# Two model blocks on one core: GpSimd arithmetic out of the first mixer, decay rows read back from DRAM, output transposed inside the last product

## The chip, the core and the metric

The kernel runs on one core of a Trainium2 chip. The core has five instruction streams: TensorE (PE, matrix products; its weight loads are shown apart as PEld), VectorE (DVE), ScalarE (ACT), GpSimd (POOL), and SyncE (SP), which here only issues transfers from device memory (DRAM) through 16 DMA engines. Operands lie in on-chip memory (SBUF) with 128 partitions; PE writes to a second memory, PSUM, which is made of banks. Each stream runs in order and waits for the others through semaphores. The metric is device time in microseconds (us), the median of several runs.

## The reference

256 tokens of width 1024 pass through two models in a row; all weights are float32.

```python
# first model, one layer
h = rmsnorm(x) * (1 + scale_m) + shift_m            # six vectors from c_act @ w_ada + b_ada
x = x + gate_m * hybrid_mixer(h)                    # retention + two gated recurrences, then w_out
x = x + gate_f * hierarchical_moe(rmsnorm(x)...)    # 32 experts, two chosen per token
x = rmsnorm(x)
# second model: layer 0 (state space mixer + dilated attention, then a gated feed-forward),
# layer 1 (conformer convolution, then a gated feed-forward); six vectors per layer as above
a_cs = cumsum(dt * A)                               # per head, inside chunks of 128 tokens
decay = exp(where(causal, a_cs[l] - a_cs[s], -inf))
y = (C B^T * decay) @ (x * dt) + (carried state)    # 32 heads, 2 chunks
return rms_norm(x, final_norm_g)
```

## The kernel before

All activations lie with the features on the partitions and the 256 tokens along the free axis. Weights stream in as 1 MB tiles (`rawa`, five buffers, loaded by SP in a fixed order); each 128x1024 piece is split by ACT (`whi`, line 211) and DVE (`wlo`, line 212) into a rounded part and a remainder, and each product takes three PE instructions per 128x128 block (lines 653 to 655 in `dense_B`, 727 to 729 in `dense_A`). Order is written out by hand: generators in a list `pipes` are advanced by one step ("tick") at fixed places of a dense product, twice in each 128-column tile of `z`, so the side work of the mixers is interleaved with the products' instructions. There is no scheduler behind it: an instruction that waits holds up all behind it on its engine.

**The first mixer** runs from about 40 to 264 us: products `fg`, `gq`, `vt`, `rqk`, `gate`, with the recurrences (`recur`), `retention` and `rotate` as side work. `recur` computes exponentials into a tile `X` (ACT) and multiplies seven levels of it by `gq` (DVE, line 976) and by `gk` (POOL, line 977); then 32x32 products on PE, whose results DVE masks (lines 1007 to 1011) and ACT copies (lines 1016 to 1018). `rotate` multiplies by sine (DVE, 902) and by cosine (POOL, 903) and adds the two (DVE, 904). Between the tiles the six modulation vectors are computed. For one third of the first model's (set (0, 2)) this is done in `ada_pooled`: POOL multiplies a 1 MB tile by the vector and adds it up in four instructions (lines 491 to 495), then two small PE products (line 503) sum over the partitions. All other sets go through `ada`: four PE products of 128x512 per tile (line 524).

**The experts** follow: their weights go to nine buffers `rawb`, which lie where the first mixer's tiles lay, so their loads can't start before the mixer has ended, and to the five `rawa` buffers.

**The state space mixer** of the second model is side work of the product `z` (16 tiles, n = 0 to 15, about 640 to 742 us): `ssd(j)` handles two heads. For each pair POOL spreads the log decays over a matrix (`Lm`, line 1720), PE forms the running sums with a triangular constant (line 1740; the second chunk's alone, line 1728), ACT takes exponentials (`M`, `e`, lines 1742 and 1744), DVE multiplies with the group's C B^T (`cbm`, line 1745), and PE forms the output (1751) and what the first chunk hands on (1753), from a third copy `xe` (POOL, 1734). DVE then combines (1754 to 1757), multiplies by the gate (`yz`, 1760), and splits the result with ACT (1768, 1769); POOL adds up squares (1762, 1764).

**The end**: after the last product `dn1`, mean square, reciprocal root (`rsqrt`, lines 606 to 611, on DVE), the root spread along the free axis by PE (`along`, 617), eight multiplications (2137), sixteen PE transposes (2143), four copies (2145, 2147) and two DMAs to the output.

Of the kernel before, what the change touches and what calls it, by code (L numbers as in the profile page):

```python
# [269 lines left out]
def _trace(ctx, tc, A, out, dbg, stop):  # L270
# [63 lines left out]
    more = spread([(0, 1, i) for i in range(8)] + [k for i in range(8) for k in ((0, 2, i), (1, 0, i))])  # L334
# [152 lines left out]
    def ada_pooled(l, b, q):  # L487

        raw = ws.get(("ada", l, b, q))
        col = 0 if l == 0 else 8  # L490
# [3 lines left out]
        t = const.tile([128, T], FT, name="sq", tag="sq", bufs=2)  # L494
        G.tensor_tensor(t, raw[:, 0], raw[:, 1], op=OP.add)
        ws.free(("ada", l, b, q))
        bias = vcol["b_ada"] if l == 0 else vcol["ada_b_2"][:, 48 * l - 48:48 * l]
        n = b * 16 + 2 * q

        def end():  # L500
            ps = mis()
            for j in range(2):
                P.matmul(ps[:, j:j + 1], t[:, j * 128:(j + 1) * 128], ones_1, start=True, stop=True)
            V.tensor_tensor(mods[l][:, n:n + 2], ps[:, 0:2], bias[:, n:n + 2], op=OP.add)
        later(9 if l else 8, end)
# [452 lines left out]
    def recur(u, heads, voff0, ot0, i):  # L958
# [13 lines left out]
        for li, m in enumerate(LEVELS):  # L972
# [4 lines left out]
            G.tensor_tensor(xv[:, :, :, 0, :], xv[:, :, :, 0, :], kv[:, :, :, 0, :], op=OP.mult)  # L977
# [548 lines left out]
    def ffn(l, mod, gain, sq, fill):  # L1526
        with ExitStack() as lx:
# [34 lines left out]
        return sq  # L1562

    with ExitStack() as l2:
# [151 lines left out]
        def ssd(j):  # L1716

            g, yj = j // 4, y[j // 4][:, j % 4]
            Lm = wk.tile([128, 2, 2, 128], FT, name="Lm", tag="Lm", bufs=2)
            G.tensor_tensor(Lm, SLb[:, None, None].to_broadcast([128, 2, 2, 128]),  # L1720
                            dA[:, :, 2 * j:2 * j + 2][:, :, :, None].to_broadcast([128, 2, 2, 128]), op=OP.mult)
            yield True
            yield True
# [441 lines left out]
```

## Time and profile before

| | us |
|---|---|
| median of 3 runs | 1557.94 |
| lowest, highest | 1554.55, 1560.27 |
| profiled execution | 1556.02 |
| its span, first to last instruction | 1554.2 |
| PE busy in it | 1380.5 (89%) |
| DVE busy | 898.1 (58%) |
| ACT busy | 633.0 (41%) |
| POOL busy | 359.2 (23%) |

The span is what the trace covers; 1.8 us lie around it. Busy times of different engines overlap. PE is the engine with the least slack, but its share is a mean over stages with different limits: in the experts' stage it waits for weights, in the feed-forward products it never stops.

### The profile page before, as it was taken

Reading aid. Unit: us, or ns where it says so; the run is one execution under the profiler, and the core shown is the slowest. Engines: PE = TensorE matmul, PEld = TensorE weight load, DVE = VectorE, ACT = ScalarE, POOL = GpSimd, SP = SyncE. Lnnn points to the kernel's source line nnn. Section 1 sums busy time; section 2 is a strip of 40 time slices with the busy share of each in tenths; the row PEclk is TensorE's granted clock in tenths of the full one; section 3 lists DMA queues with packets and bytes.
Section 4 is the critical chain, followed back from the end, with each engine's and each line's share of the span. In section 5 each row is a group of like instructions: output and inputs, shape, how many; then the busy total and the mean of one; then the engine's idle time right before and its main releaser. Section 6 shows DMA issues by size and latency. Waiting matters only on the chain.

```text
span 1554.2 us, 29404 instructions
## 1 busy us (share of the span) xinstructions
PE 1380.5 (89%) x12145; PEld 1184.7 (76%) x12145; DVE 898.1 (58%) x1683; ACT 633.0 (41%) x1117; POOL 359.2 (23%) x402
## 2 busy tenths in 40 slices
PE   3978699796687689999998899999999998999997
PEld 1757578763343389888997786899998887899997
DVE  3676666631112287877664566665555787765544
ACT  2633223320101257544443454454443766554432
POOL 3163642100000011154256203900000574000000
PEclk9998789896978889999999899999999999999998
DMA  8883456979999985655799976776557564877540
GB/s 309 295 284 125 154 163 217 361 293 418 374 417 419 359 140 152 209 180 170 178 179 168 234 200 204 208 207 178 174 182 217 177 190 136 244 193 188 176 150 28
DMA packets 283613, 344.00 MB, mean 221 GB/s; under 512 B 18249, under 2 KB 258368, under 8 KB 265552
## 3 DMA queue, kind: packets, MB, share of 16 engines
q1 hardware_dynamic: 272016, 335.33, 67.9%
q0 software_dynamic: 10848, 5.33, 3.5%
q8 instruction: 97, 1.59, 0.4%
q10 hardware_dynamic: 608, 1.39, 0.2%
q14 instruction: 44, 0.36, 0.1%
HBM read 340.63 MB, written 1.10 MB: 220 GB/s over the span
## 4 chain that ended last, share of the span: by engine, by line
PE 51%; DMA 9%; DVE 7%; ACT 3%; POOL 2%; issue 2%; POOLq 0%; SPq 0%; DVEq 0%; ACTq 0%
PE acc L653 14%; PE acc L654 14%; PE acc L655 14%; DMA rawa<-in_hy_w_in_dram 3%; DMA rawb<-in_expert_w_up_dram 3%; DVE wlo L212 2%; PE adaps L524 2%; POOL c L2029 1%; PE acc L1407 1%; DMA rawb<-in_expert_w_gate_dram 1%; PE mis L1740 1%; DMA rawa<-in_expert_w_up_dram 1%; DMA rawa<-in_expert_w_gate_dram 1%; ACT whi L211 1%; DVE q L1695 1%
## 5 line engine op out<-in xcount | busy, mean ns | idle before, releaser
L212 DVE TENSOR_TENSOR wlo<-rawa,whi 128x1024 fp32r<-128x1024 f32 (+1 forms) x303 | 378.2, 1252 | 252.2 <-ACT whi L211 251.4
L653 PE MATMUL acc<-hhi,whi 128*128 128x256 f32 (+2 forms) x1728 | 513.7, 297 | 9.4 <-ACT hhi L643 5.4
L654 PE MATMUL acc<-hlo,whi 128*128 128x256 f32 (+2 forms) x1728 | 500.0, 289 | 1.6 <-DVE hlo L649 1.2
L655 PE MATMUL acc<-hhi,wlo 128*128 128x256 f32 (+2 forms) x1728 | 498.1, 288 | 0.1
L653 PEld LDWEIGHTS acc<-hhi,whi 128*128 128x128 f32 (+2 forms) x1728 | 338.6, 196 | 45.1 <-issue 24.0
L211 ACT ACTIVATE whi<-rawa 128x1024 fp32r<-128x1024 f32 (+1 forms) x304 | 313.5, 1035 | 145.1 <-PE acc L654 105.2
L654 PEld LDWEIGHTS acc<-hlo,whi 128*128 128x128 f32 (+2 forms) x1728 | 338.9, 196 | 5.0 <-DVE hlo L649 4.2
L655 PEld LDWEIGHTS acc<-hhi,wlo 128*128 128x128 f32 (+2 forms) x1728 | 339.3, 196 | 0.5 <-DVE wlo L212 0.3
L653 PE MATMUL acc<-ghi,whi 128*128 128x256 f32 x352 | 99.6, 283 | 0.0
L654 PE MATMUL acc<-glo,whi 128*128 128x256 f32 x352 | 99.6, 283 | 0.0
L655 PE MATMUL acc<-ghi,wlo 128*128 128x256 f32 x352 | 99.6, 283 | 0.0
L1407 PE MATMUL acc<-rawb,X 128*32 128x256 f32 x576 | 63.9, 459 | 18.7 <-DMA rawb<-in_expert_w_gate_dram 10.9
L524 PE MATMUL adaps<-rawa,cs 128*32 128x512 f32 (+1 forms) x576 | 69.9, 587 | 6.0 <-DMA rawa<-in_w_ada_dram 6.0
L1979 POOL TENSOR_SCALAR dg<-cst,pcols 128x128 f32<-128x128 f32 x75 | 53.1, 726 | 84.1 <-PE acc L655 84.1
L1415 DVE TENSOR_TENSOR sq<-sq,acc 128x256 f32<-128x256 f32 x8 | 3.4, 421 | 117.0 <-PE acc L1407 117.0
L653 PEld LDWEIGHTS acc<-ghi,whi 128*128 128x128 f32 x352 | 67.6, 192 | 0.0
L654 PEld LDWEIGHTS acc<-glo,whi 128*128 128x128 f32 x352 | 67.6, 192 | 0.0
L655 PEld LDWEIGHTS acc<-ghi,wlo 128*128 128x128 f32 x352 | 67.6, 192 | 0.0
L1407 PE MATMUL acc<-rawa,X 128*32 128x256 f32 x320 | 45.4, 514 | 20.5 <-DMA rawa<-in_expert_w_up_dram 9.9
L1407 PEld LDWEIGHTS acc<-rawb,X 128*32 128x32 f32 x576 | 28.3, 131 | 43.3 <-DMA rawb<-in_expert_w_gate_dram 16.0
L1471 POOL TENSOR_TENSOR X<-X 128x256 f32<-128x256 f32 x5 | 3.9, 782 | 235.9 <-ACT X L1468 235.6
L1793 POOL DMA_DIRECT2D bt<-rbd x64 | 50.8, 806 | 31.7 <-DMA bt<-rbd 30.2
(598 smaller groups left out, 2415.0 us busy)
## 6 DMA issues: line engine op xcount, KB each, us to landing
rawa<-in_ada_w_dram SPq DMA_DIRECT2D x48, 1024.0 KB, 5.1
rawa<-in_w_ada_dram SPq DMA_DIRECT2D x24, 1024.0 KB, 8.2
rawa<-in_ffn_w_gate_dram SPq DMA_DIRECT2D x44, 512.0 KB, 4.0
rawa<-in_ffn_w_up_dram SPq DMA_DIRECT2D x44, 512.0 KB, 5.3
rawa<-in_hy_w_in_dram SPq DMA_DIRECT2D x20, 1024.0 KB, 7.4
rawa<-in_hy_w_in_dram SPq DMA_DIRECT2D x40, 512.0 KB, 7.5
rawb<-in_expert_w_gate_dram SPq DMA_DIRECT2D x18, 1024.0 KB, 19.9
rawb<-in_expert_w_up_dram SPq DMA_DIRECT2D x18, 1024.0 KB, 16.2
```

The source lines that it names most:

```text
L211: self.nc.scalar.activation(hv, src, AF.Copy)
L212: (engine or self.nc.vector).tensor_tensor(lv, src, hv.bitcast(FT), op=OP.subtract)
L524: P.matmul(ps[32 * g:32 * g + 32, :], cs[:, col + k:col + k + 1].to_broadcast([128, 32]), raw[:, k, g * w:(g + 1) * w], start=(q + k == 0) ...
L653: P.matmul(ps, wh, xh, start=start, stop=False)
L654: P.matmul(ps, wh, xl, start=False, stop=False)
L655: P.matmul(ps, wl, xh, start=False, stop=stop)
L1407: P.matmul(ps[32 * i:32 * i + 32, :256], X[:, kt, o:o + 32], half(raws[i], kt // 4)[:, kt % 4 * 256:kt % 4 * 256 + 256], start=(kt == 0), ...
L1695: V.scalar_tensor_tensor(a_[:, s_:], ps[:, :T - s_], cw[:, i:i + 1], a_[:, s_:], op0=OP.mult, op1=OP.add)
L1740: P.matmul(sg_[:, o:o + 128], Lm[:, c, a], Ub, start=True, stop=True)
L1793: nc.gpsimd.dma_start(bt[:, a, o + 64 * g:o + 64 * g + 64], bass.AP(tensor=rbd.tensor, offset=base + 511 + 127 * g, ap=[[0, 2], [1, 64], [ ...
L1979: G.tensor_scalar(diag[n][:, i], ident, tap(i, n), None, op0=OP.mult)
L2029: G.tensor_tensor(c2, c2, pr_, op=OP.add)
```

## The change

Three stages are rewritten. In the first mixer, set (0, 2) of the modulation goes through `ada` like the others, the `gk` multiplication moves from POOL to DVE, and `rotate` multiplies by cosine on DVE. In `ssd` the running sums of all heads are computed once in `softplus`, written to DRAM (`cumd`), and read back two heads at a time as rows repeated over the 128 partitions (`load_rows`, a POOL-issued DMA of 256 KB, two pairs ahead); decays come from them by an added bias, a maximum and an exponential. `Lm`, `xe`, the products 1728, 1740 and 1753 and the combination 1754 and 1757 are gone; two extra exponentials, two maxima on ACT, two on DVE, a 128x256 product on DVE and two on PE come in. At the end the gain is multiplied and the tile transposed inside `dn1`, tile by tile, and the root is applied as a per-token scale in the copies out of PSUM.

```diff
-    POOLED = {(0, 2)}
-    more = spread([(0, 1, i) for i in range(8)] + [k for i in range(8) for k in ((0, 2, i), (1, 0, i))])
+    more = spread([(l, b, i) for l, b in ((0, 1), (0, 2), (1, 0)) for i in range(8)])
-    def ada_pooled(l, b, q):
-        raw = ws.get(("ada", l, b, q))
...
-        G.tensor_tensor(raw, raw, cs[:, col:col + 8, None].to_broadcast([128, 8, 256]), op=OP.mult)
-        G.tensor_tensor(raw[:, 0:4], raw[:, 0:4], raw[:, 4:8], op=OP.add)
-        G.tensor_tensor(raw[:, 0:2], raw[:, 0:2], raw[:, 2:4], op=OP.add)
...
-        G.tensor_tensor(t, raw[:, 0], raw[:, 1], op=OP.add)
...
         P.matmul(p2[:, :T], cc("pm"), q, start=True, stop=True)
-        t1 = tmp("t1")
-        V.tensor_tensor(t1, p2[:, :T], sinT, op=OP.mult)
-        G.tensor_tensor(q, q, cosT, op=OP.mult)
-        V.tensor_tensor(rqk[:, n], t1, q, op=OP.add)
+        V.tensor_tensor(p2[:, :T], p2[:, :T], sinT, op=OP.mult)
+        V.tensor_tensor(rqk[:, n], rqk[:, n], p2[:, :T], op=OP.add)
...
         S.activation(q, ps[:, :T], AF.Copy)
+        V.tensor_tensor(rqk[:, n], ps[:, :T], cosT, op=OP.mult)
...
-            G.tensor_tensor(xv[:, :, :, 0, :], xv[:, :, :, 0, :], kv[:, :, :, 0, :], op=OP.mult)
+            V.tensor_tensor(xv[:, :, :, 0, :], xv[:, :, :, 0, :], kv[:, :, :, 0, :], op=OP.mult)
...
+            for c in range(2):
+                P.matmul(ps[:, 32 + 32 * c:64 + 32 * c], Ub, dA[:, c], start=True, stop=True)
+                P.matmul(ps[:32, 128 + 128 * c:256 + 128 * c], dA[:, c], Ub, start=True, stop=True)
+            V.tensor_copy(cum, ps[:, :96].rearrange("p (c h) -> p c h", c=3))
...
+            S.activation(pdt, ps[:32, 128:384], AF.Copy, scale=-1.0)
+            nc.gpsimd.dma_start(cumd, pdt)
+            rows.extend(load_rows(j) for j in range(2))
...
+        def load_rows(j):
+            tag, bufs = (("M", MB), ("Lm", 2))[j % 3 // 2]
+            R = wk.tile([128, 2, 2, 128], FT, name="R", tag=tag, bufs=bufs)
+            nc.gpsimd.dma_start(R.rearrange("p a c t -> p (a c t)"), bass.AP(
+                tensor=cumd.tensor, offset=cumd.offset + 2 * j * T, ap=[[0, 128], [1, 2 * T]]))
+            return R
...
-            Lm = wk.tile([128, 2, 2, 128], FT, name="Lm", tag="Lm", bufs=2)
-            G.tensor_tensor(Lm, SLb[:, None, None].to_broadcast([128, 2, 2, 128]),
...
-            yield True
+            M = rows.popleft()
+            if j < 14:
+                rows.append(load_rows(j + 2))
+            M01 = wk.tile([128, 2, 128], FT, name="M01", tag="M01", bufs=2)
+            for a in range(2):
+                h = 2 * j + a
+                S.activation(M01[:, a], M[:, a, 1], AF.Exp, bias=cum[:, 0, h:h + 1], scale=-1.0)
+                for c in range(2):
+                    if a:
+                        S.activation(M[:, a, c], M[:, a, c], AF.Relu, bias=cum[:, 1 + c, h:h + 1])
+                    else:
+                        V.tensor_scalar(M[:, a, c], M[:, a, c], cum[:, 1 + c, h:h + 1], 0.0, op0=OP.add, op1=OP.max)
+            yield True
+            S.activation(M, M, AF.Exp, scale=-1.0)
             yield True
...
-            for a in range(2):
-                P.matmul(pe[64 * a:64 * a + 64, 256:384], dA[:, 1, 2 * j + a:2 * j + a + 1].to_broadcast([128, 64]), Ub,
-                         start=True, stop=True)
...
-                    P.matmul(sg_[:, o:o + 128], Lm[:, c, a], Ub, start=True, stop=True)
...
-            S.activation(M, sg_.rearrange("p (c a t) -> p c a t", c=2, a=2), AF.Exp)
...
-            S.activation(e1, pe[:, 256:384], AF.Exp)
-            V.tensor_tensor(M, M, cbm[:, g, 0::2][:, :, None].to_broadcast([128, 2, 2, 128]), op=OP.mult)
+            V.tensor_tensor(M, M, cbm[:, g, 0::2][:, None].to_broadcast([128, 2, 2, 128]), op=OP.mult)
+            V.tensor_tensor(M01, M01, cbm[:, g, 1][:, None].to_broadcast([128, 2, 128]), op=OP.mult)
...
-            P.matmul(py[:, 256:384], xe, cbm[:, g, 1], start=True, stop=True)
-            V.tensor_tensor(e1, e1, py[:, 256:384], op=OP.mult)
+            for a in range(2):
+                P.matmul(py[64 * a:64 * a + 64, 128:256], xd[:, 0, 64 * a:64 * a + 64], M01[:, a], start=False,
+                         stop=True)
...
-            V.tensor_tensor(yt[:, 128:], yt[:, 128:], e1, op=OP.add)
...
+            turned_ = [mis() for _ in range(4)] if fin is not None else []
...
+                if fin is not None:
+                    xg = wk.tile([128, T], FT, name="xg", tag="t0", bufs=2)
+                    V.tensor_scalar(xg, xT[:, n], fin[:, n:n + 1], None, op0=OP.mult)
+                    later(2, lambda: turn_out(n, xg))
...
-        rst = rstd_of(sq)
-        for k in range(8):
-            V.scalar_tensor_tensor(xT[:, k], xT[:, k], vcol["final_norm_g_2"][:, k:k + 1], rst, op0=OP.mult, op1=OP.mult)
+        ps = acc()
+        sq.mean(ps)
+        r = rsqrt(ps[:, 0:2])
...
+            S.activation(ot[:, :512], turned_[2 * c], AF.Copy, scale=r[:, c:c + 1])
+            V.tensor_scalar(ot[:, 512:], turned_[2 * c + 1], r[:, c:c + 1], None, op0=OP.mult)
+            (nc.scalar if c else nc.sync).dma_start(out[0, c * 128:(c + 1) * 128, :], ot)
```

How this moves instructions is seen best on the two engines that PE waits for. On DVE in the first mixer, where `X` of the second recurrence is multiplied, seven rows stood between `X<-X,gq` and the masking of the 32x32 products:

```order
L971 TENSOR_TENSOR X<-X,gq 128x128
L976 TENSOR_TENSOR X<-X,gq 128x2x64
L976 TENSOR_TENSOR X<-X,gq 128x2x2x32
L976 TENSOR_TENSOR X<-X,gq 128x2x4x16
L976 TENSOR_TENSOR X<-X,gq 128x2x8x8
L976 TENSOR_TENSOR X<-X,gq 128x2x16x4
L976 TENSOR_TENSOR X<-X,gq 128x2x32x2
L976 TENSOR_TENSOR X<-X,gq 128x2x64
L1007 TENSOR_TENSOR dt__1003<-mis,l1c 128x384
```

With the change the same stretch of DVE holds both multiplications (its last rows; line numbers are those of the changed file, where 976 is 949 and 1007 is 980):

```order
L949 TENSOR_TENSOR X<-X,gq 128x2x8x8
L950 TENSOR_TENSOR X<-X,gk 128x2x8x8
L949 TENSOR_TENSOR X<-X,gq 128x2x16x4
L950 TENSOR_TENSOR X<-X,gk 128x2x16x4
L949 TENSOR_TENSOR X<-X,gq 128x2x32x2
L950 TENSOR_TENSOR X<-X,gk 128x2x32x2
L949 TENSOR_TENSOR X<-X,gq 128x2x64
L950 TENSOR_TENSOR X<-X,gk 128x2x64
L980 TENSOR_TENSOR dt__1002<-mis,l1c 128x384
```

So fourteen DVE instructions stand ahead of the masking in place of seven. On ACT in `z`, one step before (from the split of a pair's result, `yh`, to the next weight piece, `whi`; `t` is the tile's own evacuation):

```order
L1768 ACTIVATE yh_7725<-yz,pcols 128x256
L1773 ACTIVATE t_9143<-acc 128x256
L1742 ACTIVATE M<-mis 128x512
L1744 ACTIVATE e_9173<-mis 128x128
L211 ACTIVATE whi_9191<-rawa 128x1024
```

and with the change:

```order
L1768 ACTIVATE yh_7689<-yz,pcols 128x256
L1736 ACTIVATE R<-R 128x512
L1773 ACTIVATE t_8962<-acc 128x256
L1729 ACTIVATE M_8984<-R,cum 128x128 x2
L1732 ACTIVATE R<-R,cum 128x128 x2
L211 ACTIVATE whi_9004<-rawa 128x1024
```

The large exponential now stands ahead of the tile's evacuation instead of behind it, and the two small ones and the maxima, which read the rows from DRAM, stand ahead of the weight split.

## Rows read from the trace of the kernel before

**Rows 1.** windows: stretch, length, busy PE PEld DVE ACT POOL, PEclk, DMA share, GB/s

```profile
100.00:200.00 100.00, 71.40 (x1171) 57.79 (x1161) 67.88 (x85) 26.43 (x71) 52.19 (x37) 0.80 0.46 145
200.00:264.00 64.00, 59.93 (x635) 48.49 (x634) 48.09 (x81) 18.12 (x41) 28.33 (x16) 0.89 0.58 188
264.00:530.00 266.00, 197.63 (x1835) 123.72 (x1835) 73.37 (x193) 38.09 (x67) 5.64 (x7) 0.83 0.94 382
640.00:740.00 100.00, 100.00 (x848) 82.03 (x848) 76.24 (x143) 44.20 (x86) 46.25 (x60) 1.00 0.56 180
```

**Rows 2.** longest waits of PE from 40 to 240 us: total, times, longest

```profile
PE acc L727 <- ACT vtok L929: 13.1, 1, 13.1
PE mis L1072 <- DVE rqk L904: 9.7, 1, 9.7
...
PE mis L944 <- DVE mt L1074: 2.4, 1, 2.4
```

**Rows 3.** timeline of DVE, 100 to 125 us: start, duration, instruction

```profile
101.60 3.69 DVE L970 TENSOR_TENSOR X<-X,gk 128x128 f32<-128x128 f32 x1
...
105.41 8.68 DVE L976 TENSOR_TENSOR X<-X,gq 128x128 f32<-128x128 f32 x7
```

**Rows 4.** timeline of POOL in the same stretch

```profile
100.56 4.58 POOL L491 TENSOR_TENSOR rawa<-rawa,cs 128x2048 f32<-128x2048 f32 x1
```

**Rows 5.** line 976 alone: durations in ns, least/median/most

```profile
L976 DVE TENSOR_TENSOR X<-X,gq x28: 278/570/3687, 91.9 to 189.1; 128x128 f32<-128x128 f32 x28
```

**Rows 6.** line 904 alone, likewise

```profile
L904 DVE TENSOR_TENSOR rqk<-t,rq x6: 425/654/3809, 85.0 to 213.7; 128x256 f32<-128x256 f32 x6
```

**Rows 7.** timeline of DVE, 180 to 230 us

```profile
183.11 8.46 DVE L976 TENSOR_TENSOR X<-X,gq 128x128 f32<-128x128 f32 x7
...
224.88 2.45 DVE L607 TENSOR_SCALAR nw<-nw 128x12 int32<-128x12 int32 x1
```

**Rows 8.** timeline of SyncE's DMA queue, 262 to 268 us

```profile
263.76 3.98 SPq L183 DMA_DIRECT2D rawb<-in_expert_w_gate_dram  x4
```

**Rows 9.** timeline of PE in `z`, 679 to 692 us

```profile
679.30 1.06 PE L524 MATMUL adaps<-rawa,cs 128*32 128x512 f32 x8
...
683.35 0.66 PE L1751 MATMUL mis<-M,xd 128*64 128x128 f32 x8
683.94 0.49 PE L1753 MATMUL mis<-cbm,xe 128*128 128x128 f32 x2
684.26 0.38 PE L1726 MATMUL mis<-cst,y 128*128 128x128 f32 x2
684.57 0.44 PE L1728 MATMUL mis<-cst,dA 128*64 128x128 f32 x4
...
685.86 0.36 PE L653 MATMUL acc<-hhi,whi 128*128 128x256 f32 x1
...
691.58 1.06 PE L524 MATMUL adaps<-rawa,cs 128*32 128x512 f32 x8
```

**Rows 10.** timeline of all engines at the end of the program

```profile
1542.41 0.16 DVE L611 SCALAR_TENSOR_TENSOR nw<-nw 128x2 f32<-128x2 f32 x1
...
1549.44 0.69 DVE L2145 COPY ot<-mis 128x512 f32<-128x512 f32 x1 [1.01 <-PE mis L2143]
```

**Rows 11.** groups of instructions by line: busy us in all, mean ns of one

```profile
L503 PE MATMUL mis<-epsc,sq 128*128 128x1 f32 x32 | 4.7, 252 | 0.0
```

**Rows 12.** timeline of DVE in `z`

```profile
677.73 0.48 DVE L1769 SCALAR_TENSOR_TENSOR ylo<-yz,pcols,yh 128x256 fp32r<-128x256 f32 x1 [0.58 <-ACT yh L1768]
...
678.47 0.28 DVE L1754 TENSOR_TENSOR e<-e,mis 128x128 f32<-128x128 f32 x1
```

**Rows 13.** line 1745 alone, least/median/most ns

```profile
L1745 DVE TENSOR_TENSOR M<-M,cbm x16: 691/798/1068, 644.1 to 735.9; 128x512 f32<-128x512 f32 x16
```

**Rows 14.** timeline of ACT in `z`

```profile
679.40 0.60 ACT L1742 ACTIVATE M<-mis 128x512 f32<-128x512 f32 x1 [1.44 <-PE mis L1740]
```

**Rows 15.** line 1789, attention bias loads issued by POOL

```profile
DMA to landing us min/median/max: 5.8/10.3/12.9
```

More of the change, by code (lines that the diff above doesn't have):

```diff
@@ L309, in plan_ada @@
         w, c = ada_w[l], b * 2048
-        if (l, b) in POOLED:
-            src, shape = w[:, c + kt * 256:c + kt * 256 + 256].rearrange("(k p) n -> p k n", p=128), (8, 256)
-        elif (l, b) in HALVED:
+        if (l, b) in HALVED:
             h, q = divmod(kt, 4)
@@ L485, in _trace @@
     ada_ps = {}
-    def ada_pooled(l, b, q):
-        raw = ws.get(("ada", l, b, q))
-        col = 0 if l == 0 else 8
-        G.tensor_tensor(raw, raw, cs[:, col:col + 8, None].to_broadcast([128, 8, 256]), op=OP.mult)
-        G.tensor_tensor(raw[:, 0:4], raw[:, 0:4], raw[:, 4:8], op=OP.add)
-        G.tensor_tensor(raw[:, 0:2], raw[:, 0:2], raw[:, 2:4], op=OP.add)
-        t = const.tile([128, T], FT, name="sq", tag="sq", bufs=2)
-        G.tensor_tensor(t, raw[:, 0], raw[:, 1], op=OP.add)
[L496 to L505, printed above, removed]
     def ada(l, b, kt):
-        if (l, b) in POOLED:
-            ada_pooled(l, b, kt)
-            return
         h = 2 if (l, b) in HALVED else 1
@@ L533, in ada_ends @@
     def ada_ends(l, b, kt):
-        return (l, b) not in POOLED and kt % (4 if (l, b) in HALVED else 8) == (3 if (l, b) in HALVED else 7)
+        return kt % (4 if (l, b) in HALVED else 8) == (3 if (l, b) in HALVED else 7)
     def ada_end(l, n, w, sb):
@@ L1524, in _trace, with ffn @@
     hl1.close()
-    def ffn(l, mod, gain, sq, fill):
+    def ffn(l, mod, gain, sq, fill, fin=None):
         with ExitStack() as lx:
@@ L1645, in softplus @@
             P.matmul(ps[:, :32], cc("SLk"), dA[:, 0], start=True, stop=True)
-            S.activation(dec, ps[:, :32], AF.Exp)
-        dec = wk.tile([128, 32], FT, name="dec")
+            for c in range(2):
+                P.matmul(ps[:, 32 + 32 * c:64 + 32 * c], Ub, dA[:, c], start=True, stop=True)
+                P.matmul(ps[:32, 128 + 128 * c:256 + 128 * c], dA[:, c], Ub, start=True, stop=True)
+            V.tensor_copy(cum, ps[:, :96].rearrange("p (c h) -> p c h", c=3))
+            pdt = wk.tile([32, T], FT, name="pdt", tag="t1", bufs=2)
+            S.activation(pdt, ps[:32, 128:384], AF.Copy, scale=-1.0)
+            nc.gpsimd.dma_start(cumd, pdt)
+            rows.extend(load_rows(j) for j in range(2))
+        cum = wk.tile([128, 3, 32], FT, name="cum")
+        cumd = dr.tile([32, T], FT, name="cumd")
+        rows, MB = deque(), 4
+        def load_rows(j):
[4 more added lines that the diff above has]
+            return R
         y = [wk.tile([128, 4, T], FT, name="y", tag="y4", bufs=5) for _ in range(4)]
@@ L1718, in ssd @@
             g, yj = j // 4, y[j // 4][:, j % 4]
-            Lm = wk.tile([128, 2, 2, 128], FT, name="Lm", tag="Lm", bufs=2)
-            G.tensor_tensor(Lm, SLb[:, None, None].to_broadcast([128, 2, 2, 128]),
-                            dA[:, :, 2 * j:2 * j + 2][:, :, :, None].to_broadcast([128, 2, 2, 128]), op=OP.mult)
+            M = rows.popleft()
[5 more added lines that the diff above has]
+                S.activation(M01[:, a], M[:, a, 1], AF.Exp, bias=cum[:, 0, h:h + 1], scale=-1.0)
+                for c in range(2):
+                    if a:
+                        S.activation(M[:, a, c], M[:, a, c], AF.Relu, bias=cum[:, 1 + c, h:h + 1])
+                    else:
+                        V.tensor_scalar(M[:, a, c], M[:, a, c], cum[:, 1 + c, h:h + 1], 0.0, op0=OP.add, op1=OP.max)
             yield True
+            S.activation(M, M, AF.Exp, scale=-1.0)
             yield True
@@ L1821, in scores @@
                 for a, ps in enumerate(pss):
-                    s = wk.tile([128, 384], FT, name="s", tag="M", bufs=4)
+                    s = wk.tile([128, 384], FT, name="s", tag="M", bufs=MB)
                     st = wk.tile([128, 4], FT, name="st", tag="st", bufs=4)
```

31 lines of the change are left out of this document (8 added, 23 removed).

## The prediction

> **What bounds the kernel now.** I first cut the program into its stages with the view of stretches, because the shares of the whole hide different limits. Between 100 and 200 us, in the first mixer, PE is busy 71.4 of 100 us at a mean granted clock of 0.80, the DMA engines 46%; from 200 to 264 us PE is busy 59.9 of 64 at 0.89; DVE and POOL are both half busy or more [rows 1]. So neither PE nor the transfers set this stage: 28.6 + 4.1 = 32.7 us are idle, and 71.4 x 0.20 + 59.9 x 0.11 = 20.9 us of PE's busy time are lost to the clock. The view of waits says to whom: 13.1 us in one wait for the evacuation of `vtok` by ACT, 9.7 us for `rqk` of DVE, 2.4 us for `mt` of DVE [rows 2].
>
> I followed the first of these back on the timelines. ACT stood behind copies that need DVE's masking, and DVE spent 101.60 to 114.09 us on lines 970 to 976: 3.69 us in one instruction, 8.68 us in seven [rows 3], while POOL worked on a modulation tile [rows 4]. These are not slow instructions in themselves: line 976 takes 0.278 us at best and 3.687 at worst on the same shape [rows 5], line 904 from 0.425 to 3.809 [rows 6]. The long ones lie where POOL runs a long one. The same is seen ahead of the second wait, 8.46 us for seven, and in a tiny 128x12 instruction of `rsqrt` that takes 2.45 [rows 7]. The Trainium skill (SBUF — State Buffer, "SBUF: two separate sides") says that DVE and GpSimd share one pair of ports and that whoever starts holds it for the whole instruction when the DVE instruction reads two SBUF operands. The trace agrees: 3.69 us of DVE beside 4.58 us of POOL.
>
> Whether a shorter mixer shortens the program is read from what follows. The experts' loads are issued from 263.76 us on, when the mixer's memory falls free [rows 8], and from there to 530 us the DMA engines are busy 94% [rows 1]. That stage is bound by transfers whose start hangs on the mixer's end, so it should move as a block.
>
> In `z` (640 to 740 us) PE is busy without a gap at full clock [rows 1]; two steps, with one modulation tile, take 691.58 - 679.30 = 12.28 us, a step 6.14 [rows 9]. At the end, 1542.57 us (last instruction of `rsqrt`) to 1550.13 (last copy) is a chain with nothing beside it [rows 10].
>
> **The change, part by part.** *First mixer.* POOL's long instructions leave. DVE's `X` block becomes fourteen multiplications at most 0.278 each, 3.9 us, with the two before them some 4.5 in all. At the first wait that replaces 12.5 us: 8.0 saved of 13.1. At the second, 8.46 becomes 3.9 (4.6 saved), and line 904, at worst 3.81, becomes 0.43 (3.4): 8.0 of 9.7. At the third `rsqrt` gets its 2.3 back. The gain is 18.3 us of idle time. The clock fell around these waits; if the loss goes in the proportion of the idle time, 18.3/32.7 of 20.9 is 11.7 us; I take that, with nothing and all of 20.9 as ends. Against it: eight modulation tiles go to PE at 1.06 us each [rows 9], 8.5 us, while line 503 with 4.7 us leaves [rows 11]: 3.8 us more. The third instruction of `rotate` on DVE (0.43 six times) lies on an engine that is then far from full, and costs nothing unless DVE is again late at `rqk`. Sum 18.3 + 11.7 - 3.8 = 26.2 us. Bounds: 14.5 with no clock given back, about 40 where nearly every wait goes.
>
> *State space stage.* On PE a step loses line 1753 (684.26 - 683.94 = 0.32 us) and lines 1728 and 1740 (685.86 - 684.57 = 1.29), and gains two products like the four of line 1751 (0.59 / 2 = 0.30) [rows 9]: 1.31 us less, 4.83 a step, 21.0 us in sixteen. But then DVE is next. It is busy 76.2 us in 100 [rows 1], 4.68 a step. Lines 1754 and 1757 leave (0.28 each), the two maxima on 128 columns cost at most the same; the 128x256 product costs 0.42, as line 904 at its best [rows 6]; without POOL's `Lm` the product with `cbm` comes nearer its best, 0.69 for 0.80 [rows 13]. That is 4.99, and 0.58 us are DVE's wait for ACT between `yz` and `ylo` [rows 12], which stays: 5.57 a step. DVE can end the stage about one step behind PE (5 us, 0.3 a tile) and make it up under the next product, where it only splits weights. So 5.27, and 16 x 0.87 = 13.9 us saved. The upper bound is PE's 21. The lower bound is nothing: the large exponential (0.60 on ACT [rows 14]) now stands between `yh` and the tile's evacuation, and if all of it is added to DVE's loop the step is 6.17.
>
> The rows come by POOL-issued DMA, an operation the stage did not have. They are asked for two steps ahead, some 10.5 us. The nearest row is the bias loads of 129 KB, which land after 5.8 to 12.9 us, median 10.3, under a much fuller DMA [rows 15]; in `z` the engines are 56% busy [rows 1], so I take the lower end for 256 KB in long pieces, 6 us, and no wait. By the formula of the Trainium skill (DMA: Bandwidth & Descriptors, "Anatomy of one DMA — SWDGE (gpsimd) path") it would be an estimated 2.6 us; its 2.3 us for the bias loads is far under what the trace shows, so the rows decide. Either leaves this sum as it is. What is queued behind a late row on ACT is the weight split, and PE waits for that.
>
> *End.* From the root to the last copy there remain two copies on each of ACT and DVE, 2 x 0.69 = 1.4 us in place of 7.56 [rows 10]: 6.1 saved. But the transposes enter a product in which PE has no gap: a pair costs 0.31 (684.57 - 684.26 [rows 9]), six pairs 1.9; the last two pairs and the multiplication by the gain come before the mean, about 1.0. Net 3.2 us; bounds 2 and 6.
>
> **Sum.** 26.2 + 13.9 + 3.2 = 43.3 us from the profiled execution's 1556.0 gives 1512.7. The median of the runs shown is 1.9 above that execution; I add half of it and forecast 1514.
>
> **The rivals.**
> - *The first mixer finds its next wait, or the clock is not given back.* In favour: the chains ACT-DVE-PE there are long, and a copy that waits holds up the evacuations behind it. Against: three waits hold 25 us of the 33. The mixer gives 14.5: 1525.
> - *DVE and ACT set the step in `z`*, as in the lower bound above. For: the order of ACT; against: the maxima and splits may hide in the slack. `z` gives 0 to 5: 1523 to 1528. With the first rival together, about 1537.
> - *The mixer's gain is lost before the experts.* If the expert loads did not start sooner, the time would be 1540. Against it stands that their start is a release of memory [rows 8].
> - *More than I count:* nearly all idle time and clock of the first mixer come back and `z` runs at PE's 4.83: about 1490.
> - *The other side: rows that land late.* With a landing time of L the step can't be under L / 2. At 12.9 us it is 6.45, `z` loses 5 us and the time is about 1532. It is slower than before once 16 x (L/2 - 6.14) exceeds the 29.4 us saved elsewhere, L over 16 us; at 20 us the time would be 1589. For: POOL writes these transfers, 14 of them between its own squares. Against: 56% of DMA. A rule that speaks for it: the Trainium skill (SBUF — State Buffer, "SBUF: two separate sides") warns that DVE instructions of a certain kind keep GpSimd from writing descriptors, so that its transfers start late. No row here shows that.
>
> **How the numbers follow.** Chances: forecast 0.52; next wait or clock 0.14; DVE and ACT in `z` 0.14; more than counted 0.08; lost before the experts 0.05; rows late at 1532 or so 0.04, past 16 us 0.03. The range 1496 to 1538 leaves out most of the fourth, the fifth and the last. Half a per cent, 7.8 us, is about what a measurement of this kernel tells from no change. All cases but the last are faster by more than that; I keep 0.05 of their chance for a mixture of gains too small to tell.
>
> **What would show it.** Right: no DVE instruction over 1.5 us between 100 and 240 us, the waits for `vtok` and `rqk` under 5 us, expert loads issued near 238 us; `z` steps of about 5.3 us with short PE gaps; under 2 us from the root to the last copy. Wrong: PE waits of like size at new places of the mixer; ACT idle in `z` for a transfer of `R`; the experts' stage longer by what the mixer gave.

## The result, and the profile after

Twice, against runs of the kernel before on the same chip, the changed kernel took 1517.5 us (median of four, 1512.5 to 1522.6; ratio 0.9735, 95% interval 0.9704 to 0.9767) and, in the second comparison, 1518.0 us (median of five; 0.9764, 0.9741 to 0.9788). It is faster by about 2.5%, 37 to 41 us by the two ratios. The execution profiled below is a long one: 1522.6 us, span 1520.8, granted clock 0.942, where before it was 1554.2 and 0.928.

The view of stretches of the changed kernel (columns as in [rows 1]; the second and third stretch end where the first mixer and the experts now end):

```profile
100.00:200.00 100.00, 91.80 (x1613) 70.31 (x1613) 53.51 (x128) 32.27 (x87) 0.20 (x1) 0.91 0.55 189
200.00:237.00 37.00, 36.25 (x303) 28.94 (x302) 23.15 (x57) 14.74 (x29) 0.00 (x0) 1.00 0.68 230
237.00:504.00 267.00, 195.13 (x1839) 123.53 (x1843) 73.32 (x192) 38.15 (x67) 5.65 (x7) 0.85 0.94 381
624.00:724.00 100.00, 92.46 (x821) 79.00 (x820) 80.93 (x179) 63.97 (x141) 36.71 (x52) 1.00 0.74 229
```

Between 100 and 200 us, in the mixer, PE is busy 91.8 us where it was 71.4, and the granted clock is 0.91, not 0.80. The experts are as full of transfers as before, 0.94 and 381 GB/s: a block that only moved. In `z` PE was busy without a gap before; now it is not. The waits of PE in the mixer, which answer to [rows 2], and the durations of the multiplications that stood in [rows 5, 6] (line 949 is the `gq` one, 950 the `gk` one):

```profile
PE acc L701 <- ACT vtok L902: 3.8, 1, 3.8
PE mis L1045 <- DVE rqk L876: 2.1, 1, 2.1
```

```profile
L949 DVE TENSOR_TENSOR X<-X,gq x28: 284/290/297, 93.4 to 173.4; 128x128 f32<-128x128 f32 x28
...
L876 DVE TENSOR_TENSOR rqk<-rqk,mis x6: 420/422/422, 86.5 to 193.5; 128x256 f32<-128x256 f32 x6
```

The two great waits are down from 13.1 to 3.8 and from 9.7 to 2.1, and no multiplication of `X` by `gq` lasts longer than 0.297 us, where the longest took 3.687 (by `gk`, 0.299 at most). SyncE's queue tells what that gave the stage behind, as in [rows 8]:

```profile
236.83 0.34 SPq L183 DMA_DIRECT2D rawb<-in_expert_w_gate_dram  x1
```

The first expert load is issued 26.9 us earlier. The experts' end and the start of `xbc` come 26 us earlier too. But the last evacuation of `xbd` (the copy of a finished product out of PSUM) comes only 15.1 us earlier. The evacuations of `xbc` and `xbd`, before and after:

```profile
L1691 ACT ACTIVATE q<-acc,pcols x24: 545/552/566, 561.3 to 635.5; 128x256 f32<-128x256 f32 x24
```

```profile
L1695 ACT ACTIVATE q<-acc,pcols x24: 543/548/567, 535.2 to 620.4; 128x256 f32<-128x256 f32 x24
```

From the first to the last they take 85.2 us for 74.2: something took 11 us back there. PE's waits from 550 to 660 us show one of 8.4 us that was not there before, and POOL's timeline shows where it comes from:

```profile
PE mis L1688 <- DMA t<-in_consts_dram: 8.4, 1, 8.4
```

```profile
593.12 0.50 POOL L1637 DMA_DIRECT2D cumd<-pdt  x1 [20.84 <-ACT pdt L1636]
598.03 1.12 POOL L1649 DMA_DIRECT2D R<-cumd  x2 [4.41 <-DMA cumd<-pdt]
599.14 0.52 POOL L1682 DMA_DIRECT2D t<-in_consts_dram  x1
599.65 0.50 POOL L1683 DMA_DIRECT2D zs<-in_consts_dram  x1
...
```

POOL writes the running sums to DRAM at 593.12, then stands 4.41 us at the first read until that write has landed, and only behind the two reads does it issue the two constants (`t`, `zs`) of the next part of the relative bias. PE has the product with them, line 1688, next in its program from 598 us on. Before, the same loads went out at 588 to 608 us with nothing between them. And the wait costs more than itself; PE's timeline and the stretches around it:

```profile
597.63 0.28 PE L629 MATMUL acc<-hhi,wlo 128*128 128x256 f32 x1
606.34 0.60 PE L1688 MATMUL mis<-t,rel 32*16 32x127 f32 x2 [8.44 <-DMA t<-in_consts_dram]
...
607.25 0.41 PE L628 MATMUL acc<-hlo,whi 128*128 128x256 f32 x1
...
```

```profile
594.00:606.00 12.00, 3.90 (x33) 3.70 (x31) 8.45 (x15) 5.92 (x10) 3.74 (x7) 0.77 0.78 259
606.00:611.00 5.00, 4.66 (x22) 4.25 (x23) 1.41 (x2) 0.00 (x0) 0.00 (x0) 0.53 0.42 127
611.00:624.00 13.00, 13.00 (x111) 13.00 (x110) 9.21 (x16) 7.76 (x14) 0.00 (x0) 1.00 0.41 139
```

Behind the wait each product takes 0.41 us, up to 610.5 us, where at full clock (ahead of the wait) it takes 0.28; in the 5 us that follow, the granted clock is 0.53, near the lower of the two levels (1.2 of 2.4 GHz). Then it is 1.00.

In `z` a step is 5.31 us (`yz` at 667.42 to `yz` at 678.05 are two, 10.63); DVE's timeline, which answers to [rows 12], and ACT's, which answers to [rows 14]:

```profile
667.42 0.42 DVE L1760 TENSOR_TENSOR yz<-yt,zs 128x256 f32<-128x256 f32 x1
668.42 0.48 DVE L1769 SCALAR_TENSOR_TENSOR ylo<-yz,pcols,yh 128x256 fp32r<-128x256 f32 x1 [0.58 <-ACT yh L1768]
669.22 0.42 DVE L1775 SCALAR_TENSOR_TENSOR zs<-t,acc 128x256 f32<-128x256 f32 x1 [0.31 <-ACT t L1773]
669.55 0.48 DVE L1757 SCALAR_TENSOR_TENSOR yt<-y,dsk,mis 128x256 f32<-128x256 f32 x1
669.95 0.42 DVE L1742 TENSOR_TENSOR xd<-mis,dts 128x256 f32<-128x256 f32 x1
670.28 0.68 DVE L1744 TENSOR_TENSOR R<-R,cbm 128x512 f32<-128x512 f32 x1
670.88 0.42 DVE L1745 TENSOR_TENSOR M<-M,cbm 128x256 f32<-128x256 f32 x1
671.21 0.48 DVE L1734 TENSOR_SCALAR R<-R,cum 128x128 f32<-128x128 f32 x2
671.60 1.22 DVE L212 TENSOR_TENSOR wlo<-rawa,whi 128x1024 fp32r<-128x1024 f32 x1
672.74 0.42 DVE L1760 TENSOR_TENSOR yz<-yt,zs 128x256 f32<-128x256 f32 x1
```

```profile
667.88 0.51 ACT L1768 ACTIVATE yh<-yz,pcols 128x256 fp32r<-128x256 f32 x1 [1.90 <-DVE yz L1760]
668.30 0.61 ACT L1736 ACTIVATE R<-R 128x512 f32<-128x512 f32 x1
668.82 0.36 ACT L1773 ACTIVATE t<-acc 128x256 f32<-128x256 f32 x1
```

DVE is the loop: from `zs` to `yz` its rows stand without a gap, and before them are two idle pieces of 0.58 and 0.31 us, both for ACT. The second is new: `t` stands behind the large exponential. At the end, what stood in [rows 10] as 7.56 us is 1.45, from the end of `rsqrt`'s last instruction to that of the last copy (two copies on each of ACT and DVE):

```profile
1514.42 0.16 DVE L585 SCALAR_TENSOR_TENSOR nw<-nw 128x2 f32<-128x2 f32 x1
1514.62 1.27 ACT L2140 ACTIVATE ot<-mis,nw 128x512 f32<-128x512 f32 x2 [3.74 <-DVE nw L585]
1514.62 1.41 DVE L2141 TENSOR_SCALAR ot<-mis,nw 128x512 f32<-128x512 f32 x2
```

### The profile page after: what moved, and what is told of

Same layout as the page of the kernel before. It is cut to its first block, busy times and chain, and to the rows that moved or that the text cites. A ratio compares the mean times of both kernels' runs of the same rounds, so it can differ in the third digit from the quotient of the medians.

```text
span 1520.8 us, 29127 instructions
## 1 busy us (share of the span) xinstructions
PE 1348.5 (89%) x12025; PEld 1156.3 (76%) x12025; DVE 851.7 (56%) x1727; ACT 645.5 (42%) x1164; POOL 253.6 (17%) x321
## 4 chain that ended last, share of the span: by engine, by line
PE 49%; DMA 11%; DVE 6%; issue 4%; POOL 2%; ACT 2%; DVEq 0%; POOLq 0%; SPq 0%; ACTq 0%
PE acc L627 14%; PE acc L628 14%; PE acc L629 14%; DMA bt<-rbd 2%; DMA rawb<-in_expert_w_up_dram 2%; DMA rawa<-in_hy_w_in_dram 2%; DVE wlo L212 2%; PE adaps L498 2%; POOL c L2029 1%; DMA rawb<-in_expert_w_gate_dram 1%; DMA rawa<-in_expert_w_down_dram 1%; PE acc L1380 1%; DMA rawa<-in_expert_w_up_dram 1%; DMA rawa<-in_expert_w_gate_dram 1%; ACT whi L211 1%
## 5 line engine op out<-in xcount | busy, mean ns | idle before, releaser
L212 DVE TENSOR_TENSOR wlo<-rawa,whi 128x1024 fp32r<-128x1024 f32 (+1 forms) x303 | 370.0, 1225 | 256.2 <-ACT whi L211 253.5
L498 PE MATMUL adaps<-rawa,cs 128*32 128x512 f32 (+1 forms) x640 | 77.5, 589 | 6.0 <-DMA rawa<-in_w_ada_dram 6.0
L1380 PE MATMUL acc<-rawa,X 128*32 128x256 f32 x320 | 41.5, 451 | 21.5 <-DMA rawa<-in_expert_w_up_dram 11.4
L627 PE MATMUL acc<-yh,whi 128*128 128x256 f32 x192 | 54.8, 286 | 0.0
```

The costliest lines, as they stand in the source:

```text
L212: (engine or self.nc.vector).tensor_tensor(lv, src, hv.bitcast(FT), op=OP.subtract)
L498: P.matmul(ps[32 * g:32 * g + 32, :], cs[:, col + k:col + k + 1].to_broadcast([128, 32]), raw[:, k, g * w:(g + 1) * w], start=(q + k == 0) ...
L627: P.matmul(ps, wh, xh, start=start, stop=False)
L1380: P.matmul(ps[32 * i:32 * i + 32, :256], X[:, kt, o:o + 32], half(raws[i], kt // 4)[:, kt % 4 * 256:kt % 4 * 256 + 256], start=(kt == 0), ...
```

## The experiments

Each was timed beside the kernel before, and its ratio (with a 95% interval) is to that. Not all ran on the same chip, so between two kernels the ratios count as well as the medians.

**Each part alone.** Three kernels take one group of the diff's hunks each.

The mixer (of its hunks, the two that matter below):

```diff
-    POOLED = {(0, 2)}
...
-            G.tensor_tensor(xv[:, :, :, 0, :], xv[:, :, :, 0, :], kv[:, :, :, 0, :], op=OP.mult)
+            V.tensor_tensor(xv[:, :, :, 0, :], xv[:, :, :, 0, :], kv[:, :, :, 0, :], op=OP.mult)
```

> Only the first mixer of the change; state space stage and end as before. Theory (three independent parts, and what the mixer saves arrives at the end undiminished, because the experts' transfers start when its memory falls free): 26.5 us less than the kernel before, 1531, first expert load issued near 237 us, the experts' last product, the start of `z` and the end all 26 to 27 us earlier. Rival (part of what the mixer gives is lost again by `xbd`, whatever the state space part does): expert loads near 237 us, but `z` starts only some 15 us earlier, and the time is near 1542.

The state space part:

```diff
+            nc.gpsimd.dma_start(cumd, pdt)
+            rows.extend(load_rows(j) for j in range(2))
```

> Only the state space part of the change. Theory (the relative-bias constants stand behind the write and the reads of the running sums on POOL's queue; `xbd` loses 11 us to that, `z` and the rest of the stage gain 15): 4 us less than before, 1553, with a PE wait of some 8 us for `t` of the constants in `xbd` here too. Rival (that wait is there only because the mixer brings the stage forward): no such wait, and 14 to 15 us less than before, 1543.

The end:

```diff
+    sq, turned_ = ffn(1, mods[2], vcol["norm_ffn_g_2"][:, 8:16], sq, "n5", vcol["final_norm_g_2"])
```

> Only the end of the change: gain and transposes inside the last product. Theory: 3.5 us less than before, 1554; under 3 us between the root and the last copy where 7.6 stood, given back in part by a last product that is about 2 us longer. Rival (the last product is longer by as much as the chain behind it is shorter): no difference, 1557.

Measured: the mixer 1525.9 us (0.9809, 0.9794 to 0.9825), the state space part 1553.0 (0.9978, 0.9966 to 0.9990), the end 1552.6 (0.9976, 0.9962 to 0.9991), the kernel before beside them 1556.2. That is 30.3, 3.2 and 3.6 us less; by their intervals the last two are 1.6 to 5.3 and 1.4 to 5.9. The sum, 37.1, agrees with the whole change's 37 to 41. So, as closely as these intervals tell, the parts are independent, and the mixer's gain arrives undiminished. The state space part alone has the same wait in the same place (one row of PE's waits, line 1703 is there what 1688 is above), so it is not the earlier arrival that makes it:

```profile
PE mis L1703 <- DMA t<-in_consts_dram: 8.2, 1, 8.2
```

Its two halves can be read from its trace: from the first to the last evacuation of `xbc` and `xbd` 87.7 us where 74.2 stood before; from the first `zs` (the evacuated tile of `z`) to the last 76.0 where 85.4 stood, and from there to the first result of the product `houty` 23.3 for 27.5. In the changed kernel `z` takes the same 76.0; `zs` before and after:

```profile
L1775 DVE SCALAR_TENSOR_TENSOR zs<-t,acc x16: 408/414/417, 641.9 to 727.3; 128x256 f32<-128x256 f32 x16
```

```profile
L1775 DVE SCALAR_TENSOR_TENSOR zs<-t,acc x16: 414/421/422, 625.1 to 701.1; 128x256 f32<-128x256 f32 x16
```

**The wait in `xbd`.** Two repairs, which leave the arithmetic as it is. In the first the reads are asked for behind `xbd`:

```diff
             nc.gpsimd.dma_start(cumd, pdt)
-            rows.extend(load_rows(j) for j in range(2))
...
+        rows.extend(load_rows(j) for j in range(2))
         dense_B("z", cols256(0, 2048), 1024, xh, xl, ev_z)
```

> The changed kernel, with its first two reads of the rows asked for after the stage `xbd`, just ahead of `z`, so that the relative-bias constants stand ahead of them on POOL's queue. Theory (POOL's order alone delays the constants): the 8.4 us wait of PE for `t` and the low clock behind it vanish, 8 to 11 us less than the changed kernel, 1507 to 1510, a ratio to before of 0.967 to 0.970. Rival 1 (what `xbd` lost lies in the work added to `softplus`): no change, 1517. Rival 2 (rows asked for this late make the first step of `z` wait): the wait moves to the start of `z`, 1513 to 1518.

In the second another engine issues the constants:

```diff
-                G.dma_start(oht[:32, :n], A["consts"][:32, o + o_:o + o_ + n])
-                G.dma_start(mkt[:16, :n], A["consts"][:16, o + NREL + o_:o + NREL + o_ + n])
+                nc.scalar.dma_start(oht[:32, :n], A["consts"][:32, o + o_:o + o_ + n])
+                nc.scalar.dma_start(mkt[:16, :n], A["consts"][:16, o + NREL + o_:o + NREL + o_ + n])
```

> The changed kernel, with the relative-bias constants issued by ACT; the write of the running sums and the first two reads of the rows stay where they are, on POOL's queue. Theory (the constants are late because POOL issues them behind an instruction that waits for the write's landing): the wait of PE for `t` goes, as when the reads were moved, 5 to 8 us less than the changed kernel, 1509 to 1513. Rival (the two reads of 256 KB keep the constants waiting in the transfers, whoever issues them): PE still waits 3 to 6 us for `t`, 1515 to 1518.

Measured: 1510.5 (0.9708, 0.9694 to 0.9721) and 1509.3 (0.9687, 0.9659 to 0.9716), 7 to 9 us under the two medians of the changed kernel (4 to 12 by the ratios). In both the wait for `t` is gone and the stretch runs at full clock, as these 28 us of the first one show, with its evacuations of `xbc` and `xbd`:

```profile
580.00:608.00 28.00, 27.93 (x227) 26.93 (x228) 25.01 (x44) 17.88 (x31) 4.19 (x8) 1.00 0.72 239
```

```profile
L1694 ACT ACTIVATE q<-acc,pcols x24: 544/548/567, 528.7 to 603.6; 128x256 f32<-128x256 f32 x24
```

They take 74.9 us, in the second repair 75.4, for 85.2: all but about 1 us of the 11 is this wait with the slow clock behind it.

POOL's order was the cause: the constants need only not stand behind the instruction that waits for the write. How much of it was the late issue, and how much the two reads ahead of the constants in the transfers, neither run separates, since in both the constants are also issued ahead of the reads. The traces of the changed kernel and of the first repair allow an estimate: `t` was issued 6.0 us behind the write and landed after 7.2, in the repair 0.5 behind it and after 4.3. So some 5.5 us of the 8.4 were the late issue and some 2.9 the longer landing.

**What sets the step in `z`.** First the rows' landing, by asking for them one step ahead instead of two:

```diff
-            rows.extend(load_rows(j) for j in range(2))
+            rows.append(load_rows(0))
...
-            if j < 14:
-                rows.append(load_rows(j + 2))
+            if j < 15:
+                rows.append(load_rows(j + 1))
```

> The changed kernel, with the rows of each pair asked for one step ahead of their use, not two. Theory (a landing of 4.2 to 7.3 us, median 4.8, is hidden by two steps of 5.07 us and DVE's loop sets the step): with one step ahead most rows still land in time, `z` loses 0 to 10 us by the late ones, 1517 to 1527, and waits for `R` appear on ACT or DVE. Rival (the landing already sets the step, so a step is half of it): the step doubles to nearly 10 us, 1570 and more.

Then DVE's two idle pieces:

```diff
+            yield True
             S.activation(hi, yz, AF.Copy, scale=sgn[:, j:j + 1])
             V.scalar_tensor_tensor(lo, yz, sgn[:, j:j + 1], hi.bitcast(FT), op0=OP.mult, op1=OP.subtract)
```

> The changed kernel, with the weighting and split of a pair's result (`yh` on ACT, `ylo` on DVE) asked for half a step later in `z`, behind the tile's evacuation. Theory (DVE's loop sets the step: 4.43 us of work and two waits of 0.58 and 0.30 for ACT): the waits fall to some 0.1 to 0.2 in all, PE's own 4.7 us a step becomes the bound, `z` is 16 x 0.6 = 6 to 10 us shorter, and the time 1508 to 1512. Rival (PE's chain through the weight split, or the landing of the rows, sets the step): `z` keeps its 76 us from the first `zs` to the last, 1515 to 1519.

One step ahead: 1520.4 us (0.9757, 0.9725 to 0.9790), no different from the changed kernel within these intervals, and `z` keeps its 76.0 us. ACT waits for a row twice: 0.24 us in `z`, and 1.21 for the last pair's, behind the last `zs`. So the landing does not set the step (first fence: the reads of this run). With the split half a step later: 1512.1 us (0.9718, 0.9699 to 0.9737) beside 1518.0 for the changed kernel on the same chip, 5.9 us less, and the second fence has `zs` of this run, first and last start: 65.8 us for 76.0.

```profile
DMA to landing us min/median/max: 4.1/4.7/7.2
```

```profile
L1776 DVE SCALAR_TENSOR_TENSOR zs<-t,acc x16: 409/412/425, 622.3 to 688.1; 128x256 f32<-128x256 f32 x16
```

PE then waits nowhere between 620 and 690 us; it is busy all 70.0 of them. DVE's loop, with its waits for ACT, was the bound; PE's own is 4.6 us a steady step, 4.4 on the mean of all. Of these 10 us some 2.7 come back as a longer wait in the attention (`vv`, 6.1 for 3.4); where the rest of the difference between 10.2 and 5.9 went was not followed up.

**What made the mixer slow.** The mixer's part was divided: in one kernel only the modulation tiles leave POOL.

```diff
-    POOLED = {(0, 2)}
...
-    more = spread([(0, 1, i) for i in range(8)] + [k for i in range(8) for k in ((0, 2, i), (1, 0, i))])
+    more = spread([(l, b, i) for l, b in ((0, 1), (0, 2), (1, 0)) for i in range(8)])
```

> The kernel before with one part of the mixer's change: set (0, 2) of the modulation goes through PE as the other sets do; the multiplications of `gk` and of cosine stay on POOL. Theory 1 (the long modulation instructions on POOL, of 2.4 to 4.6 us each, stretch DVE's instructions beside them): most of the 30 us that the whole mixer part gave, some 20, so 1536. Theory 2 (POOL's multiplications of `X` stand behind the modulation tiles on POOL's queue, and PE waits for POOL, not for a stretched DVE): with nothing long left in that queue nearly all of it, 1528 to 1532. Rival (the multiplications on POOL that run beside DVE's own are what stretches them): under 10 us, 1548 or more.

In the other only the multiplications leave it (the other two instructions of `rotate` then work in place, as in the whole change):

```diff
-        G.tensor_tensor(q, q, cosT, op=OP.mult)
...
+        V.tensor_tensor(rqk[:, n], ps[:, :T], cosT, op=OP.mult)
...
-            G.tensor_tensor(xv[:, :, :, 0, :], xv[:, :, :, 0, :], kv[:, :, :, 0, :], op=OP.mult)
+            V.tensor_tensor(xv[:, :, :, 0, :], xv[:, :, :, 0, :], kv[:, :, :, 0, :], op=OP.mult)
```

> The kernel before with the other part: the multiplications of `gk` and of cosine move to DVE, the eight modulation tiles stay on POOL. Theory 1 (modulation tiles stretch DVE): DVE now has twice as many multiplications beside the same long instructions, so little or nothing is gained, 1548 to 1560, with DVE instructions of 3 us and more still there. Theory 2 (POOL's queue): nothing that PE waits for stands behind a modulation tile any more, so most of the 30 us, 1530 to 1535. Rival: as theory 2.

The changed kernel ran once more beside them:

> The changed kernel itself once more, so that the versions derived from it stand beside it on the same chip: 1515 to 1519, a ratio of 0.9735 to before.

Measured: the changed kernel 1518.0, the tiles alone 1519.4 (0.9766, 0.9746 to 0.9786), the multiplications alone 1564.2 (1.0045, 1.0027 to 1.0063): a little slower than before, 0.3 to 0.6%. Theory 2 falls, since in that last kernel no multiplication stood behind a tile on POOL's queue any more, and yet PE waited longer (16.6 us for `vtok`). Theory 1 has the mechanism, but its 1536 was far too high. The timelines of POOL and DVE in the kernel with the multiplications alone show the mechanism better than any group did:

```profile
107.27 3.65 POOL L491 TENSOR_TENSOR rawa<-rawa,cs 128x2048 f32<-128x2048 f32 x1
111.00 2.47 POOL L492 TENSOR_TENSOR rawa<-rawa 128x1024 f32<-128x1024 f32 x1
113.55 1.39 POOL L493 TENSOR_TENSOR rawa<-rawa 128x512 f32<-128x512 f32 x1
```

```profile
107.38 3.69 DVE L970 TENSOR_TENSOR X<-X,gq 128x128 f32<-128x128 f32 x1
110.99 0.28 DVE L975 TENSOR_TENSOR X<-X,gq 128x128 f32<-128x128 f32 x1
111.19 2.42 DVE L976 TENSOR_TENSOR X<-X,gk 128x128 f32<-128x128 f32 x1
113.54 0.28 DVE L975 TENSOR_TENSOR X<-X,gq 128x128 f32<-128x128 f32 x1
113.75 1.34 DVE L976 TENSOR_TENSOR X<-X,gk 128x128 f32<-128x128 f32 x1
```

POOL's long instruction ends at 110.92, the next at 113.47, the one after at 114.94. A DVE multiplication that starts beside one (107.38, 111.19, 113.75) ends 0.14 to 0.15 us behind it, at 111.07, 113.61 and 115.09; behind the first two, one of normal length (0.28) gets through as POOL passes to its next. So in these rows DVE and POOL take turns by the instruction, and the length of POOL's is what DVE pays. That agrees with the shared port pair of the Trainium skill (SBUF — State Buffer, "SBUF: two separate sides"), now seen instruction by instruction. Where POOL's instructions are short, the price is small: with the tiles gone, line 976's durations (950 there) are

```profile
L950 DVE TENSOR_TENSOR X<-X,gq x28: 277/411/608, 93.3 to 168.5; 128x128 f32<-128x128 f32 x28
```

0.411 at the median, beside 0.290 when POOL is silent and 3.687 at worst before. More than that: the tiles alone gave 38 us, the whole mixer part 30 (0.9766 and 0.9809, whose intervals do not meet). Not all of the mixer's part was a gain.

**Putting it together.** The first is the changed kernel with the reads behind `xbd` and the later split; the second has this as well:

```diff
-        V.tensor_tensor(rqk[:, n], ps[:, :T], cosT, op=OP.mult)
...
+        G.tensor_tensor(q, q, cosT, op=OP.mult)
...
-            V.tensor_tensor(xv[:, :, :, 0, :], xv[:, :, :, 0, :], kv[:, :, :, 0, :], op=OP.mult)
+            G.tensor_tensor(xv[:, :, :, 0, :], xv[:, :, :, 0, :], kv[:, :, :, 0, :], op=OP.mult)
```

> The changed kernel with both repairs: the first reads of the rows after `xbd`, and the split of a pair's result half a step later. Theory (two waits in different stages): the gains of 7 and 6 us add, 1504 to 1506, ratio 0.967. Rival (one wait stands in for the other, or the rows asked for late are now missed by the faster `z`): 1509 to 1512.

> Both repairs, and the multiplications of `gk` and of cosine back on POOL, with the modulation tiles on PE. Theory (POOL's short multiplications take work off DVE and stretch its own only from 0.28 to 0.41 us; DVE's chain ahead of the masking gets shorter by one multiplication in two): 3 to 7 us less than with both repairs alone, 1498 to 1502. Rival (the short ones stretch DVE by what they save; the lower time of that form of the mixer alone was a difference between chips): within 2 us of both repairs alone.

Measured: 1502.4 (0.9635, 0.9603 to 0.9667) and 1494.9 (0.9606, 0.9578 to 0.9633), with 1496.3 to 1504.0 and 1494.6 to 1497.3 as the ends of five runs each. The repairs add. With the multiplications on POOL the median is 7.5 us lower still, the ratio 4.5 us; the two intervals overlap, so this pair alone would not settle it, but it goes the way of the other two comparisons: 0.9766 for 0.9809 between the tiles alone and the mixer's whole part, and 1564.2 for 1557.5 where the tiles stayed on POOL. All three move `gk` and cosine together; which of the two counts was not separated. The waits of PE from 40 to 240 us in the two profiles, first with the multiplications on DVE, then on POOL:

```profile
PE acc L701 <- ACT vtok L902: 3.4, 1, 3.4
PE mis L1045 <- DVE rqk L876: 2.1, 1, 2.1
...
PE mis L1009 <- ACT hsq L1003: 1.5, 1, 1.5
```

```profile
PE acc L701 <- ACT vtok L903: 2.1, 1, 2.1
...
PE mis L1046 <- DVE rqk L878: 0.9, 1, 0.9
```

The wait at `rqk` is 0.9 for 2.1, that at `vtok` 2.1 for 3.4, and the 1.5 us at `hsq` are gone; the granted clock from 100 to 228 us is 0.99 for 0.95. The first expert load goes out at 228.60 for 236.68. This last kernel, 3.9% under the one before, is the fastest of those measured.

## Why the prediction was nearly right, point by point

*The total*, 1514 for 1517.5 and 1518.0, hides errors of opposite sign: some 6 us more gained than counted in the three parts, and 11 lost that were not counted at all. That it came within 4 us is in part luck.

*First mixer: right in kind, too small.* I had 26.2 us; alone it measured 30.3. In the profiled execution the first expert load went out 26.9 us earlier (I said near 238 us; 236.83), in the profiled executions of seven more runs with the same mixer 27.1 to 33.0 earlier. By the terms: idle time from 100 us to the first expert load is 9.0 us (8.2 + 0.8), 23.7 less, where I counted 18.3; I left the waits for `hsq` and `mod` out, which went too, all but 0.8 us. The fourteen multiplications took 0.284 to 0.299 us each; the 0.278 that I called the most was the least of [rows 5], which is 0.2 us in all. The clock gave back 20.9 - 8.3 = 12.6 us (8.3 is 91.80 x 0.09), where my proportion said 11.7. By this sum PE's work in that stretch grew by 9.4 us (23.7 + 12.6 - 26.9), where I had 3.8. The modulation is not the cause: its products take 18.3 us there for 11.3, and the 4.7 of line 503 are gone. Some 1.8 us is a group of the recurrence's products that ran just ahead of 100 us before (98.4 to 100.2) and behind it after. The remaining 5 stay open; the clock's term is itself an estimate, since a hundredth of the clock is 1.3 us over this stretch.

*The multiplications moved to DVE: wrong.* Of the third instruction of `rotate` I said that it "costs nothing unless DVE is again late at `rqk`". DVE is late there, 2.1 us (0.9 with the multiplications on POOL), and the two moves together cost 4 to 8 us by three comparisons. The whole gain was in the tiles. I gave both moves one sum because both took POOL's arithmetic away; I did not ask which of POOL's instructions had stretched which of DVE's. The rows had it: DVE's multiplications of 3 us and more lay beside POOL's tiles, and [rows 5] has 0.570 at the median beside 3.687 at worst.

*State space stage, `z`: right.* The steady step went from 6.14 to 5.31 us; I had 5.27. DVE's loop is the bound, as said: 0.58 of wait for `yh` stayed, and the new wait of 0.31 for `t` took the place of the 0.3 I had put on DVE ending behind PE. The lower bound (the whole exponential in DVE's loop) did not come: of its 0.61 us only 0.31 stand in DVE's way. By the landmarks the stage gave 15.3 us (from 15.1 earlier at the end of `xbd` to 30.4 earlier at the first result of `houty`); I had 13.9. It did not come as sixteen steps of 0.87: twelve steady steps gave 10.0 us and the three ahead of them lost 0.6, while 4.2 came behind the last `zs` and 1.7 ahead of the first. The rows landed in 4.8 us at the median, 7.3 at most, without a wait in `z`, near what I took from [rows 15]; the 2.6 us by the formula of the Trainium skill (DMA: Bandwidth & Descriptors, "Anatomy of one DMA — SWDGE (gpsimd) path") were too low here.

*What was missed: `xbd`.* The step that failed is the term for the rows' transfers, "so I take the lower end for 256 KB in long pieces, 6 us, and no wait", with the sentence near it that named only ACT as the engine on which something stands behind a late row. In `z` it held; ahead of `z` it put at nothing a term that measured 11 us. I costed the reads in `z` and left out how they begin: a write to DRAM, a wait for its landing, and then two reads, on a queue that also issues the relative bias' constants. What followed from that (a wait of 8.4 us and the slow clock behind it) took 11 of the 15 us; both repairs of POOL's order bring 10 of them back in `xbc` and `xbd`, and 7 to 9 in the whole time. Had I asked what stands behind the new instructions on POOL's queue, the order of POOL would have shown the constants there.

*End: right.* 3.6 us alone, 3.2 predicted; from the root to the last copy 1.45 us, where I had 1.4.

*The rivals.* The mixer's gain was not lost before the experts, and the rows were not late; DVE and ACT do set the step, but at 5.31, not at the 5.8 or more that this rival meant.

## What to carry to other kernels

Before arithmetic is moved off GpSimd, separate its long instructions from its short ones: here only the modulation tiles, in instructions of up to 4.6 us, were worth moving, and the multiplications of some 0.5 and 0.75 us were cheaper where they were. A DMA that reads what the same queue has just written held that queue here until the write had landed (4.4 us); look at what else the queue issues, in the stage where the write stands and not only where the data are used. When a stage's loop runs through two engines that wait for each other, moving a pair of instructions by half a step can be worth as much as the work taken out of the loop (here 10.2 us of `z` for 9.4).

## What the runs showed of the hardware that was not expected

Two vector instructions in a row beside one long GpSimd instruction don't share the loss: the first lasts to the end of GpSimd's instruction (3.69, 2.42, 1.34 us), the next takes its normal 0.28. The Trainium skill (SBUF — State Buffer, "Who interferes with whom") exempts a DVE instruction with at most one SBUF input, outside the two-port modes, and the trace agrees: in the kernel before, `t<-mis,sinT` (line 902; `mis` lies in PSUM) at 191.88 us took 0.41 us beside a POOL instruction that ran from 191.50 to 192.77. All six of that line took 0.408 to 0.425, while line 904, with two SBUF inputs of the same shape, took up to 3.809 [rows 6]. From the issue of a write of 32 KB to DRAM to the first read behind it on the same queue, 4.9 us passed (593.12 to 598.03), and 4.9 and 5.4 in the two repairs. And a wait of 8.4 us of PE was followed by 4 us of products at 0.41 us, in a stage that lost 11 in all.
